# A hybrid S5 / GLA / dilated-attention block on one Trainium2 core: three edits to the order of the work around the gate products

## The chip, the cores and the metric

The kernel runs on one core of one Trainium2 chip. The metric is the device time of one execution in microseconds (us). The core's engines are named as the profile names them: PE is TensorE (matmuls), DVE is VectorE, ACT is ScalarE, POOL is GpSimd and SP is SyncE, which here only starts DMAs. Each engine works through its own list of instructions in order and waits, where it must, for semaphores of the others.

## What is computed

The reference is one transformer block in float32, 1024 tokens of width 1024. The first half of it is what matters here; it mixes three branches:

```python
(u_s5, q_gla, k_gla, v_gla, lr_gla, r_gla, q_att, k_att, v_att, gate_logits) = split(rms_norm(x) @ w_in)
y_a = s5_branch(u_s5, ...)          # state space: per group of 16 channels, 64 complex states, scan over 1024 tokens
y_b = gla_branch(q_gla, ...)        # gated linear attention, 4 heads, chunks of 64
y_c = dilated_branch(q_att, ...)    # windowed attention with dilation 1, 4, 16
gates = sigmoid(gate_logits)        # 1024 x 3 x 1024
merged = sum(gates * einsum('bsnc,ncd->bsnd', stack([y_a, y_b, y_c]), w_branch))
x = x + merged @ w_out
```

Then come cross-attention to 256 memory rows and a squared-ReLU MLP of width 4096, which the change touches only through the stream of weights.

## The kernel before

**Products in split float32.** Large products are made of pairs: each operand is split into a first part (`whi`, `A_hi`), which is the value rounded to the matmul's reduced float32 type, and a second part (`wlo`, `A_lo`), which is what is left. `gemm` (L455) issues three matmuls for each slice of 128 of the contraction: hi x hi, hi x lo, lo x hi. In the profile these are the `m<-A_hi,whi`, `m<-A_lo,whi` and `m<-A_hi,wlo` rows of L151.

**The stream of weights** (`Stream`, L259). `load` (L283) starts on SP's queue the DMA of half a block of weights into one of three buffers `raw`. `begin` queues a block's four quarters. Each call of `tick` (L315) converts one quarter: ACT writes the first part `whi` (L140, scaled by a gain `gk`, or a plain copy at L146), and DVE then writes the second part `wlo` (L137, or L121), which reads what ACT has just written. After every second quarter, `tick` calls `load` for the buffer that came free. `next` finishes whatever quarters of a block are left and begins the following block.

**The clock of the program.** While a large product is issued, `spend` (L440) adds up the matmuls' nominal time. At every 1.28 us of it, one step is taken of each of the side jobs in `sides`, at a rate that each job has; at every second step `ws.tick()` is called. So side jobs are Python generators whose `yield` statements decide how many PE matmuls stand between two of their pieces. Six large matmuls of 512 columns (two slices of the contraction) fill one such step.

**The side jobs in this part of the program.** While the gate products (`gate_evac`, L1230, whose results go to `GT_d` through SP, L1234) run on PE:

- `gla` (from L1031) runs first. It works on pairs of chunks; a table of offsets (`GLA_LV`, `GLA_OUT`) says at which step each piece is issued. `level` makes, for seven levels, an exponential `E`, products `Kt` and `Qt` on DVE and POOL, and PE multiplies `Qt` by `Kt`. `outp` (L1143) makes the result of one chunk: `oc` scales it on DVE, `od` multiplies it by the gate `rg` on POOL, `oe` transposes it on PE, and `of` (L1183) splits it in two parts `e` and stores both to `YB_d` in memory, with DMAs issued by POOL (L1190). The last step of one pair of chunks and the first of the next overlap.
- `p2` waits for `gla` to end and runs `s5b` (L909). It loads `Ug`, the regrouped input, with eight DMAs on SP (L920), and tables (`GTr`, `GTi`, `ctab`, `stab`, `CLr`, `CLi`, `Tz`) with DMAs on POOL (L923). Then come four rounds `qd`. A round multiplies `Ug` by `GTr` and `GTi` on PE (S5's first products), rotates and scans the result on DVE (`Vr`, `Vi`, then `Xr`, `Xi`), waits two steps, and makes the output products: in two halves `q`, each of four `k`, three matmuls with `Tz`, `CLr` and `CLi`, with one `yield` between `k == 1` and `k == 2`. ACT applies the gelu (`Yg`), PE transposes, and ACT and DVE split the result into `GH`.

After the last gate block the program calls `sides.finish(sd_p2)`, which issues all that is left of `s5b` with nothing between, and then starts the next large product, which reads `GH`.

Of the kernel before, what the change touches and what calls it, by code (L numbers as in the profile page):

```python
# [12 lines left out]
ALU = mybir.AluOpType  # L13
# [4 lines left out]
P = 128  # L18
# [67 lines left out]
def body(tc, I, out):  # L86
# [55 lines left out]
    def f(ap):  # L142
        return ap.bitcast(F32)

    def split(hi, lo, src):
        S.copy(hi, src)  # L146
        sub(lo, src, f(hi))
# [114 lines left out]
    class Stream:  # L262
# [3 lines left out]

        def __init__(self):
            self.i = 0
            self.n_load = 0
            self.raw = []  # L270
            self.hl = {}
            self.todo = []

            self.sums, self.n_hi, self.n_lo, self.done, self.started = {}, 0, 0, 0, False
            self.queue7, self.sum_queue, self.parts, self.pair = [], [], {}, None
            self.rows, self.left, self.held, self.n_sum = {}, {}, [], 0
            for x in range(3):
                if x == 2:
                    p0_x(1, SP)
                self.load()  # L280
            self.begin(0)
# [16 lines left out]
        def begin(self, i):  # L298
# [13 lines left out]
            for q in range(4):  # L312
                self.todo.append((hi[:, q * n // 4:(q + 1) * n // 4], lo[:, q * n // 4:(q + 1) * n // 4], q, n // 4, gains[i], k // 4))

        def tick(self):  # L315
            if self.todo:
                hi, lo, q, n, g, nk = self.todo.pop(0)
                raw = self.raw[0][:, q % 2 * n:q % 2 * n + n]
                if g is None:
                    split(hi, lo, raw)  # L320
                else:
                    for k in range(nk):
                        c = slice(k * n // nk, (k + 1) * n // nk)
                        gk = gv[:, g, nk * q + k:nk * q + k + 1]
                        act(hi[:, c], raw[:, c], AF.Copy, scale=gk)
                        stt(lo[:, c], raw[:, c], gk, f(hi[:, c]), ALU.mult, ALU.subtract)
                if q % 2:
                    self.raw.pop(0)
                    self.load()
                return  # L330
            if self.n_lo < len(self.queue7):
                self.tick7()
            elif self.queue7 and self.done >= self.n_lo - 4 and self.i < len(blocks) and not isinstance(gains[self.i], tuple) and self.i not in self.hl:
                self.begin(self.i)
# [574 lines left out]
    def s5b(p, GH):  # L909
# [14 lines left out]
        load(0, ("Ug", "GTr", "GTi", "ctab", "stab"))  # L924
        yield
        load(0, ("CLr", "CLi", "Tz"))
        for _ in range(2):
            yield
        for qd in range(4):
            cur = got[qd]  # L930
            j0 = 4 * qd
            Ug = cur["Ug"]

            SS = []
            load(qd + 1, ("Ug",))
            for l in ("GTr", "GTi"):
                o = qtile([P, 4, P])
                for j in range(4):
                    for x in range(2):
                        mm(o[x * 64:(x + 1) * 64, j, :], cur[l][:, j, x * 64:(x + 1) * 64], Ug[:, 2 * j + x, :])  # L940
                SS.append(o)
                yield
            Sr, Si = SS
            ctab, stab = (cur[n].rearrange("p (a b) -> p a b", a=4) for n in ("ctab", "stab"))
            c1, s1 = ctab[:, :, 1:], stab[:, :, 1:]
            Vr, Vi = T(p, [P, 4, NCH], "Vr"), T(p, [P, 4, NCH], "Vi")
            va, vb = T(ev, [P, 4, NCH], "e1", bufs=2), T(ev, [P, 4, NCH], "e2", bufs=2)
            mul(Vr, Sr, c1)
            mul(vb, Sr, s1)
            mul(va, Si, s1)  # L950
            yield
            add(Vr, Vr, va, eng=G)
            mul(Vi, Si, c1)
            sub(Vi, Vi, vb)
            yield
            load(qd + 1, ("GTr", "GTi"))
            for v in (Vr, Vi):
                for j in range(4):
                    V.tensor_tensor_scan(out=v[:, j, :], data0=rho[:, j0 + j:j0 + j + 1].to_broadcast([P, NCH]),
                                         data1=v[:, j, :], initial=0.0, op0=ALU.mult, op1=ALU.add)  # L960
                yield
            load(qd + 1, ("ctab", "stab"))
            Xr, Xi = T(p, [P, 4, NCH], "Xr"), T(p, [P, 4, NCH], "Xi")
            m = NCH - 1
            c_, s_ = ctab[:, :, 1:NCH], stab[:, :, 1:NCH]
            G.memset(Xr[:, :, 0], 0.0)
            G.memset(Xi[:, :, 0], 0.0)
            mul(va[:, :, :m], Vi[:, :, :m], s_, eng=G)
            mul(vb[:, :, :m], Vi[:, :, :m], c_, eng=G)
            mul(Xr[:, :, 1:], Vr[:, :, :m], c_)  # L970
            mul(Xi[:, :, 1:], Vr[:, :, :m], s_)
            yield
            sub(Xr[:, :, 1:], Xr[:, :, 1:], va[:, :, :m])
            yield
            add(Xi[:, :, 1:], Xi[:, :, 1:], vb[:, :, :m])
            for _ in range(2):
                yield
            Yg = T(p, [P, L5, 8, 16], "Yg")
            CL = [cur[n].rearrange("p (a b) -> p a b", a=4) for n in ("CLr", "CLi")]
            for q in range(2):  # L980
                ps = qtile([P, 4, P])
                o = slice(q * 64, q * 64 + 64)
                for k in range(4):
                    mm(ps[:, k, :], Ug[:, 2 * k + q, :], cur["Tz"][:, 2 * k + q, :], stop=False)
                    mm(ps[:, k, :], Xr[o, k, :], CL[0][o, k, 16:144], start=False, stop=False)
                    mm(ps[:, k, :], Xi[o, k, :], CL[1][o, k, 16:144], start=False)
                    if k == 1:
                        yield
                act(Yg[:, :, q::2, :], ps.rearrange("p k (t c) -> p t k c", t=L5), AF.Gelu_apprx_tanh)
                yield  # L990
            gh = [x[:, qd, :] for x in GH]
            load(qd + 1, ("CLr", "CLi", "Tz"))
            for q in range(2):
                ps = qtile([P, 4, P])
                for k in range(4):
                    tr(ps[:, k, :], Yg[:, 4 * q + k].rearrange("p g c -> p (g c)"))
                hi, lo = (g_.rearrange("p (c t) -> p t c", t=L5)[:, 4 * q:4 * q + 4, :] for g_ in gh)
                split(hi, lo, ps)
                yield
# [46 lines left out]
    def gla(p, B, GQ, GK, GV):  # L1046
# [5 lines left out]
        def tpair(tp, base):  # L1052
# [89 lines left out]
            def outp(t, o0):  # L1142
# [42 lines left out]
                def of():  # L1185
                    hi = T(ev, [P, 4, P], "e1", F32R, bufs=2)
                    lo = T(ev, [P, 4, P], "e2", F32R, bufs=2)
                    split(hi, lo, r["pt"])
                    for x, y in enumerate((hi, lo)):
                        G.dma_start(YB_d[x][:, :, tg * P:(tg + 1) * P], y)  # L1190
                for i, fn in enumerate((oa, ob, oc, od, oe, of)):
                    at(o0 + GLA_OUT[i], fn)
            o0 = GLA_L0 + GLA_SP * 6 + GLA_LV[3] + 1
# [1150 lines left out]
```

## Time and profile before

| | |
|---|---|
| runs shown | 2351.93, 2352.48, 2360.95 us; median 2352.48 us |
| the profiled execution, its own time | 2361.8 us |
| its span, first to last instruction | 2360.0 us |
| PE busy | 2272.0 us, 96% of the span |
| DVE, ACT, POOL busy | 1397.6, 811.0, 635.3 us |
| mean granted clock of PE | 0.976 of full speed |

How to read it: a share of busy time is a mean over stages with different limits. Idle time of PE is what can be gained without removing matmuls, and so is time in which PE is busy at less than its full clock: `PEclk` is the clock granted to TensorE, 1.00 for 2.4 GHz and 0.50 for 1.2 GHz, and a value between them is a mean over a stretch that has both. In a row of the timeline, the brackets hold the idle time of the engine just before the instruction and what ended it.

### The profile page before, as it was taken

The page shows a single profiled execution, that of the slowest core. Times are in us where ns is not written, and L with a number is a line of the kernel's source. Part 1 is how long each engine was busy: PE and PEld are TensorE (multiplying, and loading weights), DVE is VectorE, ACT ScalarE, POOL GpSimd, SP SyncE. Part 2 cuts the span into 40 slices and gives each one's busy share as a digit, 9 for nine tenths or more (in the row PEclk, how much of TensorE's full clock was granted, in tenths as well). Part 3 has the DMA queues.
Part 4 walks back from the last instruction along what each step waited for, and adds up shares of the span by engine and source line. Part 5 has one row for each costly group of instructions (what it writes and reads, how often), then busy time and mean ns, then how long its engine had stood idle before and what let it go on. Part 6 is the DMA issues. An engine that isn't in the chain of part 4 may idle for free.

```text
span 2360.0 us, 31525 instructions
## 1 busy us (share of the span) xinstructions
PE 2272.0 (96%) x11680; PEld 1909.1 (81%) x11680; DVE 1397.6 (59%) x2514; ACT 811.0 (34%) x1777; POOL 635.3 (27%) x589
## 2 busy tenths in 40 slices
PE   9999899999999999999998999999899999999998
PEld 8778777777889888978886889899688888678787
DVE  7886986354542334353347555384577777786674
ACT  5325222112323333323223344263333334343324
POOL 3221444121210000010003320022556563454513
PEclk9999999798999999999999999999899999999999
DMA  5343235441651111141146324101044445354331
GB/s 178 108 147 90 56 88 126 136 122 68 229 157 41 40 45 44 48 90 39 38 115 217 134 66 140 45 10 45 18 147 152 149 153 167 124 177 141 106 103 72
DMA packets 201849, 246.37 MB, mean 104 GB/s; under 512 B 15424, under 2 KB 143072, under 8 KB 201696
## 3 DMA queue, kind: packets, MB, share of 16 engines
q1 hardware_dynamic: 187472, 221.35, 30.2%
q0 software_dynamic: 12640, 18.23, 2.9%
q10 hardware_dynamic: 1584, 4.78, 0.6%
q8 instruction: 92, 1.51, 0.3%
q14 instruction: 61, 0.50, 0.1%
HBM read 179.92 MB, written 64.39 MB: 104 GB/s over the span
## 4 chain that ended last, share of the span: by engine, by line
PE 73%; DVE 14%; DMA 4%; ACT 3%; issue 3%; POOL 2%; SPq 0%; DVEq 0%; ACTq 0%; POOLq 0%
PE m L151 50%; PE q L151 21%; PE q L184 2%; DVE wlo L137 2%; DVE Qt L121 1%; DVE e L121 1%; DMA fm<-ACT_d 1%; DMA wb<-W_d 1%; DVE A_lo L121 1%; POOL b L121 1%; DVE wlo L121 1%; DVE ST L1132 1%; DVE e L137 1%; DVE Kt L121 1%; ACT whi L140 1%
## 5 line engine op out<-in xcount | busy, mean ns | idle before, releaser
L151 PE MATMUL m<-A_hi,whi 128*128 128x512 f32 x1680 | 686.5, 409 | 7.7 <-DVE e L121 7.7
L151 PE MATMUL m<-A_lo,whi 128*128 128x512 f32 x1680 | 665.0, 396 | 7.4 <-POOL A_lo L121 5.2
L151 PE MATMUL m<-A_hi,wlo 128*128 128x512 f32 x1680 | 664.1, 395 | 0.0
L151 PEld LDWEIGHTS m<-A_hi,whi 128*128 128x128 f32 x1680 | 321.4, 191 | 75.4 <-DVE e L121 8.5
L151 PEld LDWEIGHTS m<-A_lo,whi 128*128 128x128 f32 x1680 | 321.8, 192 | 70.5 <-POOL A_lo L121 6.8
L151 PEld LDWEIGHTS m<-A_hi,wlo 128*128 128x128 f32 x1680 | 320.9, 191 | 69.8
L151 PE MATMUL q<-b,whi 128*128 128x512 f32 (+1 forms) x768 | 238.1, 389 | 10.4 <-ACT b L1918 4.1
L137 DVE SCALAR_TENSOR_TENSOR wlo<-raw,gv,whi 128x256 fp32r<-128x256 f32 (+1 forms) x400 | 194.5, 535 | 71.0 <-ACT whi L140 70.6
L140 ACT ACTIVATE whi<-raw,gv 128x256 fp32r<-128x256 f32 (+1 forms) x400 | 174.7, 501 | 174.0 <-PE m L151 141.4
L151 PEld LDWEIGHTS q<-b,whi 128*128 128x128 f32 x768 | 144.3, 191 | 47.3 <-POOL b L121 7.4
L121 DVE TENSOR_TENSOR wlo<-raw,whi 128x512 fp32r<-128x512 f32 x160 | 151.4, 953 | 40.0 <-ACT whi L146 29.7
L121 DVE TENSOR_TENSOR e<-m,RSB 128x512 f32<-128x512 f32 x64 | 50.2, 785 | 166.6 <-PE m L151 160.9
L151 PE MATMUL q<-b,wlo 128*128 128x512 f32 (+1 forms) x384 | 147.5, 384 | 0.0
L121 DVE TENSOR_TENSOR X<-X,q 128x512 f32<-128x512 f32 (+1 forms) x119 | 75.3, 648 | 76.3 <-PE q L151 64.8
L1415 POOL DMA_DIRECT2D ST_d<-s x6 | 3.1, 514 | 400.0 <-ACT s L1414 400.0
L121 POOL TENSOR_TENSOR RSB<-RSB,e 128x512 f32<-128x512 f32 (+1 forms) x53 | 54.6, 1030 | 204.6 <-ACT e L140 204.2
L140 ACT ACTIVATE e<-e 128x512 f32<-128x512 f32 x94 | 59.4, 633 | 137.2 <-DVE e L137 59.3
L151 PE MATMUL m<-whi,A_hi 128*128 128x256 f32 (+1 forms) x328 | 94.1, 287 | 0.0
L151 PE MATMUL m<-whi,A_lo 128*128 128x256 f32 (+1 forms) x328 | 92.9, 283 | 0.0
L151 PE MATMUL m<-wlo,A_hi 128*128 128x256 f32 (+1 forms) x328 | 92.8, 283 | 0.0
L140 ACT ACTIVATE pr<-nl,st 128x128 f32<-128x128 f32 (+1 forms) x96 | 43.3, 451 | 129.8 <-DVE st L1375 129.6
L151 PE MATMUL q<-A_lo,whi 128*128 128x512 f32 (+1 forms) x224 | 84.1, 376 | 3.9 <-POOL A_lo L121 2.6
(397 smaller groups left out, 4242.4 us busy)
## 6 DMA issues: line engine op xcount, KB each, us to landing
raw<-in_w_in_dram SPq DMA_DIRECT2D x48, 512.0 KB
fm<-ACT_d SPq DMA_DIRECT2D x68, 256.0 KB
raw<-in_w_up_dram SPq DMA_DIRECT2D x32, 512.0 KB
raw<-in_w_down_dram SPq DMA_DIRECT2D x32, 512.0 KB
GT_d<-e SPq DMA_DIRECT2D x48, 256.0 KB
raw<-in_w_in_dram SPq DMA_DIRECT2D x48, 256.0 KB
ACT_d<-e SPq DMA_DIRECT2D x48, 256.0 KB
ACT_d<-fm SPq DMA_DIRECT2D x36, 256.0 KB
```

Of the source, the lines that this page charges most:

```text
L121: return eng.tensor_tensor(out=o, in0=a, in1=b, op=op)
L137: return V.scalar_tensor_tensor(out=o, in0=a, scalar=s, in1=b, op0=op0, op1=op1)
L140: return S.activation(o, a, f, **kw)
L151: PE.matmul(o, l, r, start=start, stop=stop, skip_group_check=on_top)
L184: PE.transpose(o, a, ident[:n, :n])
L1132: V.copy_predicated(s["ST"].rearrange("p h (b x n) -> p h b x n", x=2, n=Hh)[:, :, :, 1, :], lmask[:, li * 64:(li + 1) * 64].rearrange("p ...
L1415: G.dma_start(ST_d[ip][g], s2)
```

## The change

Three edits, all in the order in which the same work is issued; no instruction of arithmetic is added or removed.

1. `s5b`: five steps in place of two between the loads and S5's first products; four steps in place of two between the scans and the output products; no step inside a half of the output products.
2. `of`: the two stores to `YB_d` are issued by SP in place of POOL, with both sides seen as plain float32.
3. `Stream.tick`: the second part of a quarter, and the `load` that follows a half block, are put into a list `behind` and issued after the first part of the next quarter. After the last quarter of a block, and in the first blocks (`self.i < 3`), the list is emptied at once.

```diff
         def tick(self):
+
             if self.todo:
+                late, self.behind = self.behind, []
                 hi, lo, q, n, g, nk = self.todo.pop(0)
                 raw = self.raw[0][:, q % 2 * n:q % 2 * n + n]
                 if g is None:
-                    split(hi, lo, raw)
+                    S.copy(hi, raw)
+                    self.behind.append(lambda: sub(lo, raw, f(hi)))
                 else:
                     for k in range(nk):
...
                         act(hi[:, c], raw[:, c], AF.Copy, scale=gk)
-                        stt(lo[:, c], raw[:, c], gk, f(hi[:, c]), ALU.mult, ALU.subtract)
+                        self.behind.append(lambda c=c, gk=gk: stt(lo[:, c], raw[:, c], gk, f(hi[:, c]), ALU.mult, ALU.subtract))
+                        if self.i < 3:
+                            self.flush()
                 if q % 2:
                     self.raw.pop(0)
-                    self.load()
+                    self.behind.append(self.load)
+                for fn in late:
+                    fn()
+                if self.i < 3 or not self.todo:
+                    self.flush()
                 return
...
         load(0, ("CLr", "CLi", "Tz"))
-        for _ in range(2):
+        for _ in range(5):
             yield
...
             add(Xi[:, :, 1:], Xi[:, :, 1:], vb[:, :, :m])
-            for _ in range(2):
+            for _ in range(4):
                 yield
...
                     mm(ps[:, k, :], Xi[o, k, :], CL[1][o, k, 16:144], start=False)
-                    if k == 1:
-                        yield
                 act(Yg[:, :, q::2, :], ps.rearrange("p k (t c) -> p t k c", t=L5), AF.Gelu_apprx_tanh)
...
                     for x, y in enumerate((hi, lo)):
-                        G.dma_start(YB_d[x][:, :, tg * P:(tg + 1) * P], y)
+                        SP.dma_start(f(YB_d[x][:, :, tg * P:(tg + 1) * P]), f(y))
```

How this moves instructions shows on three engines. First DVE's list in the first round of `s5b`, from the rotation to the first correction of `Xr`. Before:

```order
L121 TENSOR_TENSOR e_590_4138<-q_4092,stab_4047 128x512
L121 TENSOR_TENSOR e_589_4137<-q_4113,stab_4047 128x512
L137 SCALAR_TENSOR_TENSOR wlo_4059<-raw_3858,gv_82,whi_4058 128x256 x2
L121 TENSOR_TENSOR Vi_4136<-q_4113,ctab_4045 128x512
L121 TENSOR_TENSOR Vi_4136<-Vi_4136,e_590_4138 128x512
L959 SCALAR_TENSOR_TENSOR Vr_4135<-rho_155,Vr_4135 128x128 x4
L137 SCALAR_TENSOR_TENSOR wlo_4059<-raw_3858,gv_82,whi_4058 128x256 x2
L959 SCALAR_TENSOR_TENSOR Vi_4136<-rho_155,Vi_4136 128x128 x4
L121 TENSOR_TENSOR e_594_4188<-m_4131,RSB_91 128x512
L121 TENSOR_TENSOR Xr_4199<-Vr_4135,ctab_4045 128x4x127
L121 TENSOR_TENSOR Xi_4200<-Vr_4135,stab_4047 128x4x127
L121 TENSOR_TENSOR Xr_4199<-Xr_4199,e_589_4137 128x4x127
```

After the change, from the start of the rotation:

```order
L121 TENSOR_TENSOR Vr_4160<-q_4122,ctab_4045 128x512
L121 TENSOR_TENSOR e_591_4163<-q_4122,stab_4047 128x512
L121 TENSOR_TENSOR e_590_4162<-q_4137,stab_4047 128x512
L121 TENSOR_TENSOR e_592_4173<-m_4100,RSB_91 128x512
L121 TENSOR_TENSOR Vi_4161<-q_4137,ctab_4045 128x512
L121 TENSOR_TENSOR Vi_4161<-Vi_4161,e_591_4163 128x512
L973 SCALAR_TENSOR_TENSOR Vr_4160<-rho_155,Vr_4160 128x128 x4
L973 SCALAR_TENSOR_TENSOR Vi_4161<-rho_155,Vi_4161 128x128 x4
L121 TENSOR_TENSOR Xr_4214<-Vr_4160,ctab_4045 128x4x127
L121 TENSOR_TENSOR Xi_4215<-Vr_4160,stab_4047 128x4x127
L121 TENSOR_TENSOR e_600_4228<-m_4176,RSB_91 128x512
L121 TENSOR_TENSOR Xr_4214<-Xr_4214,e_590_4162 128x4x127
```

The two pairs of `wlo` have left the stretch between rotation and `Xr`; six of them now stand ahead of it, and the `e<-m` rows (gate results taken out of PSUM) fall at other places.

Next PE's list at the end of `s5b`, from the last output product of the fourth round to the first product that reads `GH`. Before:

```order
L151 MATMUL q_4974<-CLi_4790,Xi_4913 128x128
L151 MATMUL m_4946<-A_hi_101,whi_4536 128x512
L151 MATMUL m_4946<-A_lo_102,whi_4536 128x512
L151 MATMUL m_4946<-A_hi_101,wlo_4537 128x512
L151 MATMUL m_4946<-A_hi_101,whi_4536 128x512
L151 MATMUL m_4946<-A_lo_102,whi_4536 128x512
L151 MATMUL m_4946<-A_hi_101,wlo_4537 128x512
L184 MATMUL q_5003<-ident_84,Yg_4950 128x128 x4
L184 MATMUL q_5010<-ident_84,Yg_4950 128x128 x4
L151 MATMUL m_5026<-GH_567_4027,whi_4782 128x512
```

After the change:

```order
L151 MATMUL q_4989<-CLr_4806,Xr_4927 128x128
L151 MATMUL q_4989<-CLi_4808,Xi_4928 128x128
L184 MATMUL q_5003<-ident_84,Yg_4974 128x128 x4
L184 MATMUL q_5010<-ident_84,Yg_4974 128x128 x4
L151 MATMUL m_5026<-GH_567_4027,whi_4753 128x512
```

The six gate matmuls between the last output product and the transposes (`q<-ident,Yg`) are gone from there, and all 24 output products of that round stand in one run. In the first three rounds the list now has 66 gate matmuls in place of 57 between S5's first products and the output products (60 in the fourth), two runs of 12 output products with 6 gate matmuls between them in place of four runs of 6 with 3, 6 and 6 between, and 18 gate matmuls more ahead of the very first product of `s5b`.

Last SP's list where `gla` ends and `s5b` begins. Before:

```order
L1234 DMA GT_d_122<-e_553_3933 128x512
L1161 DMA rg_3940<-RG_d_120 128x512
L1234 DMA GT_d_122<-e_562_3989 128x512
L920 DMA Ug_4032<-U_d_121 16x8x128 x8
L1234 DMA GT_d_122<-e_574_4055 128x512
L920 DMA Ug_4083<-U_d_121 16x8x128 x8
```

After the change:

```order
L1246 DMA GT_d_122<-e_562_3989 128x512
L1202 DMA YB_d_28_123<-e_565_4016 512x1x128
L1202 DMA YB_d_29_124<-e_566_4017 512x1x128
L934 DMA Ug_4032<-U_d_121 16x8x128 x8
L1246 DMA GT_d_122<-e_574_4055 128x512
```

The stores of the last chunk now stand directly ahead of the first loads of `Ug`, and the second set of `Ug` loads has moved further back. POOL's list loses these stores and goes from the multiplication by `rg` straight to the loads of the tables.

## Rows read from the trace of the kernel before

**Rows 1.** Windows by stretch: length, busy us of each engine (count), PEclk, DMA share, GB/s.
```profile
228.00:244.00 16.00, 12.96 (x106) 12.38 (x106) 13.54 (x27) 5.39 (x11) 4.70 (x6) 1.00 0.23 65
280.00:300.00 20.00, 15.15 (x73) 12.25 (x72) 19.05 (x27) 4.37 (x15) 11.73 (x15) 0.91 0.42 97
325.00:345.00 20.00, 15.79 (x72) 12.83 (x71) 17.73 (x24) 4.79 (x9) 11.64 (x15) 0.83 0.35 71
370.00:380.00 10.00, 7.31 (x38) 5.75 (x37) 9.26 (x14) 1.94 (x4) 5.53 (x7) 1.00 0.45 95
410.00:425.00 15.00, 11.21 (x60) 8.51 (x60) 2.70 (x6) 3.31 (x8) 2.40 (x5) 0.77 1.01 263
435.00:465.00 30.00, 28.57 (x93) 21.99 (x93) 5.57 (x7) 4.73 (x7) 3.10 (x4) 0.60 0.24 79
480.00:500.00 20.00, 18.56 (x96) 14.64 (x95) 5.95 (x8) 2.59 (x5) 4.35 (x5) 1.00 0.30 90
515.00:545.00 30.00, 28.57 (x91) 22.01 (x91) 6.31 (x9) 1.72 (x3) 4.41 (x5) 0.60 0.24 80
560.00:580.00 20.00, 19.60 (x101) 15.56 (x100) 6.63 (x10) 2.53 (x4) 3.31 (x3) 1.00 0.16 58
```

**Rows 2.** Timeline of PE ahead of S5's first product: start us, us, instruction.
```profile
412.32 0.39 PE L151 MATMUL m<-A_lo,whi 128*128 128x512 f32 x1
412.55 0.39 PE L151 MATMUL m<-A_hi,wlo 128*128 128x512 f32 x1
416.72 0.69 PE L151 MATMUL q<-Ug,GTr 128*64 128x128 f32 x4 [3.79 <-DMA Ug<-U_d]
```

**Rows 3.** Waits of PE, 400 to 560 us: total us, times, longest.
```profile
PE q L151 <- DVE Xr L121: 4.0, 3, 1.3
```

**Rows 4.** Timeline of PE at the first output products of S5's first round.
```profile
435.95 0.38 PE L151 MATMUL q<-Tz,Ug 128*128 128x128 f32 x2
437.65 0.49 PE L151 MATMUL q<-CLr,Xr 64*128 64x128 f32 x2 [1.32 <-DVE Xr L121]
```

**Rows 5.** Timeline of DVE between rotation and Xr in that round.
```profile
426.97 1.91 DVE L137 SCALAR_TENSOR_TENSOR wlo<-raw,gv,whi 128x256 fp32r<-128x256 f32 x2
...
431.41 0.86 DVE L137 SCALAR_TENSOR_TENSOR wlo<-raw,gv,whi 128x256 fp32r<-128x256 f32 x2
```

**Rows 6.** Waits of DVE, 200 to 395 us.
```profile
DVE wlo L137 <- ACT whi L140: 11.9, 16, 1.2
```

**Rows 7.** Timeline of all engines where two pairs of GLA's chunks meet.
```profile
284.24 0.68 DVE L121 TENSOR_TENSOR e<-q,gst 128x512 f32<-128x512 f32 x1
...
285.85 1.55 POOL L1190 DMA_DIRECT2D YB_d<-e  x2 [1.82 <-ACT e L146]
...
286.78 4.66 DVE L121 TENSOR_TENSOR Kt<-E,GK 128x256 f32<-128x256 f32 x1
...
287.27 1.42 POOL L121 TENSOR_TENSOR e<-e,rg 128x512 f32<-128x512 f32 x1
...
288.74 0.66 PE L184 MATMUL q<-ident,e 128*128 128x128 f32 x4 [1.20 <-POOL e L121]
...
289.74 1.40 POOL L121 TENSOR_TENSOR e<-GQ,GK 128x512 f32<-128x512 f32 x1
...
292.35 0.98 PE L151 MATMUL q<-Qt,Kt 128*128 128x128 f32 x4 [2.95 <-DVE Qt L121]
```

**Rows 8.** Timeline of SP's queue: the first loads of Ug.
```profile
405.53 4.67 SPq L920 DMA_DIRECT2D Ug<-U_d  x8
```

**Rows 9.** Timeline of DVE: the second part of GLA's last result.
```profile
406.79 0.69 DVE L121 TENSOR_TENSOR e<-q,e 128x512 fp32r<-128x512 f32 x1 [1.78 <-ACT e L146]
```

**Rows 10.** Timeline of POOL: last multiplication by rg.
```profile
402.85 1.37 POOL L121 TENSOR_TENSOR e<-e,rg 128x512 f32<-128x512 f32 x1
```

**Rows 11.** Timeline of ACT: the last gelu of S5.
```profile
576.65 0.60 ACT L140 ACTIVATE Yg<-q 128x512 f32<-128x512 f32 x1 [6.34 <-PE q L151]
```

**Rows 12.** The page's fifth part, conversion of weights on ACT: idle before, releasers.
```profile
L140 ACT ACTIVATE whi<-raw,gv 128x256 fp32r<-128x256 f32 (+1 forms) x400 | 174.7, 501 | 174.0 <-PE m L151 141.4
```

More of the change, by code (lines that the diff above doesn't have):

```diff
@@ L268, in __init__ @@
             self.i = 0
+            self.behind = []
             self.n_load = 0
@@ L313, in begin, with flush @@
                 self.todo.append((hi[:, q * n // 4:(q + 1) * n // 4], lo[:, q * n // 4:(q + 1) * n // 4], q, n // 4, gains[i], k // 4))
+        def flush(self):
+            while self.behind:
+                self.behind.pop(0)()
         def tick(self):
             if self.todo:
+                late, self.behind = self.behind, []
                 hi, lo, q, n, g, nk = self.todo.pop(0)
```

## The prediction

> **What bounds the kernel now.** PE is busy for 96% of the span, so I looked first for the stretches in which it is not, or in which its clock is below 2.4 GHz, and then for what ended its waits there. Windows of 5 us over the whole trace led to the stretches in [rows 1]. In each I take as lost the length less busy time times mean clock; that is rough where idle time and a low clock fall together. The gate stage has two parts. While GLA's side job runs, 228 to 244 loses 3.0 us, 280 to 300 loses 20 - 15.15 x 0.91 = 6.2, 325 to 345 loses 6.9, and 370 to 380 loses 2.7. While S5's side job runs, 410 to 425 loses 6.4, 435 to 465 loses 30 - 28.57 x 0.60 = 12.9, 480 to 500 loses 1.4, 515 to 545 loses 12.9 and 560 to 580 loses 0.4. That is 18.8 us and 34.0 us; the change works on just these.
>
> In S5 the causes are short waits. PE stands 3.79 us for `Ug` [rows 2], and in rounds one to three 4.0 us in all for `Xr` [rows 3], 1.32 of it in the first round [rows 4]. The larger part is the clock that follows. In the first and third rounds it fell to 1.2 GHz a few us after the wait and stayed there while output products ran; after the same loss of 1.4 us in the second round, and with 0.4 us in the fourth, it stayed at 2.4 GHz [rows 1].
>
> **S5's first products.** They move back by 18 gate matmuls. One gate matmul follows the other after 0.23 us [rows 2], so PE arrives 4.1 us later, against a wait of 3.79. But the load moves too. Its eight DMAs started at 405.53 [rows 8]; now two stores stand ahead of them, and the second of these needs DVE's result of 406.79 + 0.69 = 407.48 [rows 9]. With about 0.58 us for one DMA's issue (4.67 / 8), `Ug` would start some 3.1 us later, and at worst 3.79 + 3.1 - 4.1 = 2.8 us of wait stay. In favour: POOL no longer waits for the same result between its multiplication, which ends at 404.22 [rows 10], and its seven table loads. Those transfers filled the DMA engines in 410 to 425 (share 1.01 [rows 1]), which is why `Ug` came late. They now leave earlier, and the second set of `Ug` leaves later. I take the wait as gone, and the lost clock of the stretch with it: 6.4 us; the other end is 1.0.
>
> **The output products.** Rounds one to three get nine more gate matmuls ahead of them, 2.1 us, against waits of 1.3 us. DVE's way to `Xr` also loses two pairs of `wlo`, 1.91 + 0.86 = 2.8 us [rows 5], whose place ahead of the rotation is one where DVE waits for PE anyway. So the waits should be gone with 3 us to spare: 4.0 and the fourth round's 0.4, with the bounds 4.4 and 3. Losing the step inside a half costs no arithmetic, but the output products now stand in runs of 12. Whether the clock then holds is the largest open term: 12.9 - 1.4 = 11.5 us for each of two rounds, 23.0 in all. Its ends are 23.0 saved, and 23.0 lost if the second and fourth rounds fall too. I take 23.0 saved, because the nearest row is 480 to 500: four runs of six, a loss of 1.4 us ahead, and clock 1.00 throughout.
>
> **The end of S5.** The fourth round now finishes with nothing between its pieces. The six gate matmuls that stood over the last gelu are used up earlier, so PE waits for that gelu: 0.60 us [rows 11] and the hand-over, which I put at 0.3 from what stands between such rows; 0.9 lost, between 0.6 and 2. Splitting `GH` was exposed before and stays so.
>
> S5 together: 6.4 + 12.9 + 12.9 + 1.4 + 0.4 - 0.9 = 33.1 us.
>
> **Second parts behind the next first part.** Between 200 and 395 us DVE stood 11.9 us, 16 times, for the first part that ACT was still writing [rows 6]. That is about 0.75 each, four times in 228 to 244, where DVE is the engine that PE waits for: 3.0 lost by PE there, four times 0.75 removed. With a quarter's second part behind the next quarter's first, ACT is done when DVE comes to it. I take all of 3.0; the ends are 1 and 3.0. Elsewhere I cost the edit at nothing. A second part is late by one tick, two steps, and conversion runs ahead: ACT's longest waits are for PE to release the buffer of the block before (141.4 of 174.0 us [rows 12]). If that cover were gone, a `raw` buffer could come late, at 1 to 3 us in a place where blocks are short.
>
> **Stores on SP.** Sixteen issues leave POOL. The price of one is seen where two pairs of chunks meet [rows 7]. DVE's result for POOL is ready at 284.24 + 0.68 = 284.92, but POOL waits for ACT's and DVE's parts, issues the two stores, and multiplies only from 287.27. From there it runs four instructions without a gap until 291.14. DVE's `Kt`, begun at 286.78, takes 4.66 us in all that time and ends 0.30 us behind POOL's run, and PE waits 1.20 and then 2.95 us. Without the stores the run begins 2.35 us earlier and so does all that follows: PE's 4.15 become 1.8. The two other meetings look the same, so 7.0 us. Their clock, 1.3 + 2.7 = 4.0, should then hold, as it did in 370 to 380 with 2.7 us idle. Together 11.0. The lower end is nothing, if the run of POOL only meets other work of DVE; the upper is all of the three windows, 15.8.
>
> As the Trainium skill has it (SBUF — State Buffer, section "SBUF: two separate sides"), VectorE with two inputs in SBUF and GpSimd exclude each other for a whole instruction, whichever starts first. If VectorE came in after the one instruction, it would have been out for no more than 1.42 us here, and only the waits of 1.20 would be saved: 3.6 in place of 7.0, and 2318. The row of 4.66 us says that the whole run of four holds it out.
>
> SP's own time costs nothing as long as it idles; what stands behind the stores there is weighed below.
>
> **Sum.** 33.1 + 3.0 + 11.0 = 47.1 us. Against the profiled execution's own 2361.8 that is 2314.7, so **2315**. That execution is 9.3 us above the median of the runs shown and near the highest of them (2360.95); against the median the forecast is a gain of 37 us.
>
> **Rivals.**
> - *The clock still falls in some rounds.* For it: `CLr` and `CLi` use half of the rows (64*128 [rows 4]), only 6 gate matmuls stand between the runs in place of 15 in a round, and in 435 to 465 the clock didn't come back until these products ended. Against it: no wait precedes them. 11.5 us a round: 2326 for one, 2338 for two. Chance 0.18.
> - *It falls in all four rounds, and the kernel is slower.* The same place and price, now caused by the runs of 12 alone: 2315 + 46 = 2361, above the median of before; with `Ug` late and the lower end of the stores it passes 2364. It decides from the fourth round on (three give 2349). Chance 0.05.
> - *DVE is held out as long as before.* POOL's run starts earlier, but only the 1.20 waits go: 11.0 becomes about 3.6, so 2322; with nothing gained, 2326. Chance 0.12.
> - *SP holds `Ug` back.* The stores wait on SP, and all loads behind them too: 2.8 us of wait and 2.6 of clock stay, 2320. Chance 0.04. The Trainium skill (DMA: Bandwidth & Descriptors, section "Anatomy of one DMA — SWDGE (gpsimd) path") says that a DMA's wait for a semaphore happens on the issuing sequencer before dispatch. By that rule this rival is certain to delay the start of `Ug`; the two times of [rows 8, 9] show the order, and not the outcome.
> - *Nothing moves the end*, because what PE saves it waits for at the next block of weights: 2352. Chance 0.03.
>
> **How the numbers follow.** The forecast has 0.58, from 2309 (all 52.8 us of the windows) to 2322. The range reaches from 2305, 4 us lower for what the third edit may save outside the windows, to 2338, two rounds at the low clock. Half a percent, about 12 us, is what a measurement of this kernel can tell from no change. Faster by more than that is below 2340.7: the forecast, most of the first rival, the third and fourth, 0.88 after taking off a little for prices that I may have wrong together. Within it 0.09, slower 0.03.
>
> **What would show it.** Right: no PE wait for `Xr`, and at most 1 us for `Ug`; clock 1.00 through S5's four rounds; DVE's waits for `whi` in the GLA part down from 11.9 to under 4 us; DVE's longest `Kt` or `Qt` under 3 us; a new PE wait of about 1 us ahead of S5's last transposes. Wrong: a clock of 0.5 inside the runs of 12 without a wait ahead; `Kt` still at 4.6 us; PE waiting for `raw` or `wlo`.

## The result, and the profile after

The changed kernel takes **2321.67 us** (median of four executions, 2317.44 to 2324.36) against 2353.8 us before (four, 2351.93 to 2360.95): ratio 0.9848, 95% interval 0.9826 to 0.987. That is faster by 1.5%, inside the forecast's range and 6.7 us above its 2315. The executions that left the two profiles took 2361.8 and 2317.4 us: 44.4 us apart, where the sum had said 47.1.

The windows that answer to [rows 1] lie up to 40 us earlier now (columns as there):

```profile
228.00:244.00 16.00, 15.20 (x130) 15.02 (x129) 15.82 (x33) 4.13 (x8) 6.82 (x9) 1.00 0.23 67
274.00:294.00 20.00, 17.39 (x102) 14.48 (x101) 19.10 (x33) 6.34 (x18) 10.55 (x13) 1.00 0.40 127
313.00:333.00 20.00, 17.34 (x100) 14.44 (x99) 19.14 (x32) 6.34 (x18) 10.61 (x13) 1.00 0.41 127
353.00:365.00 12.00, 10.73 (x57) 8.66 (x57) 11.13 (x22) 3.19 (x12) 6.22 (x8) 1.00 0.45 132
398.00:413.00 15.00, 12.54 (x78) 9.79 (x77) 6.51 (x13) 0.63 (x2) 3.54 (x7) 1.00 0.92 250
420.00:440.00 20.00, 20.00 (x115) 15.79 (x114) 4.71 (x7) 7.42 (x12) 1.65 (x3) 1.00 0.24 82
455.00:475.00 20.00, 20.00 (x115) 15.52 (x115) 5.39 (x9) 6.68 (x12) 1.64 (x3) 1.00 0.25 83
488.00:508.00 20.00, 20.00 (x115) 15.78 (x114) 4.50 (x7) 5.57 (x8) 1.65 (x3) 1.00 0.25 83
520.00:540.00 20.00, 19.31 (x94) 15.53 (x93) 5.86 (x7) 6.16 (x8) 1.19 (x2) 0.91 0.07 26
```

S5's first three rounds lose nothing: PE is busy for the whole window at clock 1.00, where two rounds before lost 12.9 us each. The meetings of GLA's chunks lose 2.6, 2.7 and 1.3 us in place of 6.2, 6.9 and 2.7. What is left in S5 is 2.46 us ahead of its first products and 20 - 19.31 x 0.91 = 2.4 us at its end.

The waits of PE, 400 to 560 us (against [rows 3]), and DVE's wait for the first part, 200 to 395 us (against [rows 6]):

```profile
PE q L151 <- DMA GT_d<-e: 2.5, 1, 2.5
PE q L184 <- ACT Yg L140: 0.7, 1, 0.7
...
DVE wlo L137 <- ACT whi L140: 0.8, 1, 0.8
```

No wait for `Xr` is left, and DVE's 11.9 us for `whi` are 0.8. The first row names a store, but the waiting matmul reads `Ug` and `GTr`, and `GTr` and `GTi` had landed by 396.3; so it waits for `Ug`. SP's queue (columns: start, us) and SP's own waits, 388 to 412 us, tell why:

```profile
392.07 1.24 SPq L1202 DMA_DIRECT2D YB_d<-e  x2
393.49 8.97 SPq L934 DMA_DIRECT2D Ug<-U_d  x8
402.57 0.84 SPq L1246 DMA_DIRECT2D GT_d<-e  x2
...
404.77 1.09 PE L151 MATMUL q<-Ug,GTr 128*64 128x128 f32 x16 [2.46 <-DMA GT_d<-e]
```

```profile
SPq L934 <- DMA YB_d<-e: 2.6, 2, 2.2
```

The two stores are issued, then the eight loads of `Ug`, which need 8.97 us to issue where they needed 4.67 [rows 8]. Of these, 2.6 us are waits of SP: by this row the seventh and the eighth load stand until the two stores ahead of them are done. PE arrives at 404.77 - 2.46 = 402.31 and waits. But from the first load's issue to the first product it is 11.28 us here, and it was 416.72 - 405.53 = 11.19 before [rows 2, 8]: `Ug` needs no longer than it did. What moved is the time that PE leaves it: PE now arrives 8.82 us after the first issue, and 7.40 before.

Where the first two pairs of chunks meet, DVE and POOL (against [rows 7]):

```profile
279.36 0.68 DVE L121 TENSOR_TENSOR e<-q,gst 128x512 f32<-128x512 f32 x1
280.12 1.29 POOL L121 TENSOR_TENSOR e<-e,rg 128x512 f32<-128x512 f32 x1 [0.96 <-DVE e L121]
...
281.37 0.74 POOL L121 TENSOR_TENSOR Kt<-E,GK 128x256 f32<-128x256 f32 x1
281.91 0.49 DVE L121 TENSOR_TENSOR Kt<-E,GK 128x256 f32<-128x256 f32 x1
282.07 0.80 POOL L121 TENSOR_TENSOR E<-B 128x256 f32<-128x256 f32 x1
282.32 2.26 DVE L121 TENSOR_TENSOR Qt<-E,GQ 64x256 f32<-64x256 f32 x2
282.83 1.46 POOL L121 TENSOR_TENSOR e<-GQ,GK 128x512 f32<-128x512 f32 x1
```

POOL multiplies 0.08 us after DVE's result is ready (279.36 + 0.68), where it took 2.35 us before. `Kt` takes 0.49 us in place of 4.66.

### The profile page after: what moved, and what is told of

The parts are those of the page before. It is cut to its first block, busy times and chain, and to the rows that moved or that the text cites. A ratio compares the mean times of both kernels' runs of the same rounds, so it can differ in the third digit from the quotient of the medians.

```text
span 2315.7 us, 31549 instructions
## 1 busy us (share of the span) xinstructions
PE 2241.2 (97%) x11680; PEld 1888.9 (82%) x11680; DVE 1383.6 (60%) x2514; ACT 811.0 (35%) x1777; POOL 627.8 (27%) x573
## 5 line engine op out<-in xcount | busy, mean ns | idle before, releaser
L151 PE MATMUL m<-A_hi,whi 128*128 128x512 f32 x1680 | 678.3, 404 | 9.3 <-DVE e L121 9.3
L151 PE MATMUL m<-A_lo,whi 128*128 128x512 f32 x1680 | 658.1, 392 | 6.8 <-POOL A_lo L121 3.5
L151 PEld LDWEIGHTS m<-A_hi,whi 128*128 128x128 f32 x1680 | 317.7, 189 | 74.6 <-DVE e L121 10.2
L137 DVE SCALAR_TENSOR_TENSOR wlo<-raw,gv,whi 128x256 fp32r<-128x256 f32 (+1 forms) x400 | 188.7, 525 | 14.2 <-ACT whi L140 14.1
```

The lines of the kernel that those rows point to most:

```text
L137: return V.scalar_tensor_tensor(out=o, in0=a, scalar=s, in1=b, op0=op0, op1=op1)
L151: PE.matmul(o, l, r, start=start, stop=stop, skip_group_check=on_top)
```

## The experiments

Ratios are to the kernel before, run beside each group (medians 2358.25, 2361.68 and 2358.51 us of 17, 7 and 9 executions), with 95% intervals. The four kernels with ratios to 2361.68 ran on another chip, and the changed kernel was not among them: they compare with it through the ratios (0.9848 and 0.9842 for the changed kernel). "Lost" is length less busy time times clock, as in the prediction.

### The parts alone

S5's steps alone (the first edit):

```diff
-        for _ in range(2):
+        for _ in range(5):
...
-            for _ in range(2):
+            for _ in range(4):
...
-                    if k == 1:
-                        yield
```

> The kernel before with the steps of S5 alone (five steps, four steps, none inside a half); stores on POOL and second parts as before. Theory: the three edits work on separate stretches and their gains add. Between 400 and 585 us the kernel before lost 34.8 us to waits and low clock, the changed one 4.7, so this kernel gains 28 to 32 us against the profiled execution of before: ratio 0.986 to 0.989. The wait for Ug is gone or under 1 us, because POOL's stores, not SP's, stand ahead of the tables; no wait for Xr in rounds one to three; clock 1.00 there. The three meetings of GLA's chunks stay as before (18.8 us lost from 228 to 380). Rival: the second parts of weights, still between rotation and Xr on DVE, keep PE waiting for Xr for 0.5 us or more a round, and the dense runs of output products behind that wait lose the clock in one round or more: gain 7 to 20 us, ratio 0.991 to 0.997.

Measured 2329.97 us, ratio 0.9885 (0.9868 to 0.9901), as the theory had it: no wait for `Xr`, clock 1.00 in the rounds, 0.5 us for `Ug`, the meetings as before.

The stores alone (the second edit):

```diff
-                        G.dma_start(YB_d[x][:, :, tg * P:(tg + 1) * P], y)
+                        SP.dma_start(f(YB_d[x][:, :, tg * P:(tg + 1) * P]), f(y))
```

> The kernel before with the sixteen stores of GLA's result on SP alone. Theory: the meetings of two pairs of chunks lose 6.5 us in place of 15.8, no product Kt or Qt on DVE is over 2.5 us, and their clock stays at 1.00; but SP's loads of Ug now wait behind two stores and PE comes to S5's first products 4.1 us earlier than in the changed kernel, so its wait for Ug grows from 3.8 to 6 or 7 us. Net gain 5 to 9 us, ratio 0.996 to 0.998. Rival: the products on DVE became short because second parts of weights left its list there, not because of the stores; then the longest Kt stays at 4.6 us, the meetings lose 13 us or more, and with the longer wait for Ug the kernel is equal or slower, ratio 1.000 to 1.002.

Measured 2352.46 us, ratio 0.9977 (0.9963 to 0.9991). The three meetings of chunks (windows):

```profile
280.00:295.00 15.00, 12.36 (x67) 9.87 (x66) 14.21 (x24) 3.34 (x7) 8.58 (x10) 1.00 0.35 103
320.00:335.00 15.00, 12.36 (x69) 10.16 (x68) 13.82 (x21) 4.16 (x8) 7.96 (x10) 1.00 0.30 91
355.00:365.00 10.00, 8.68 (x50) 6.96 (x48) 9.15 (x19) 2.77 (x11) 5.47 (x7) 1.00 0.52 155
```

The waits of PE, 200 to 600 us:

```profile
PE q L151 <- DMA Ug<-U_d: 6.8, 1, 6.8
```

The theory held. The meetings lose 2.6, 2.6 and 1.3 us, as in the whole change: the stores, not the second parts, cause that gain. The wait for `Ug` grows from 3.8 to 6.8 us, the other side of the same edit.

The second parts alone (the third edit; the core of its diff stands ahead of the prediction):

```diff
-                        stt(lo[:, c], raw[:, c], gk, f(hi[:, c]), ALU.mult, ALU.subtract)
+                        self.behind.append(lambda c=c, gk=gk: stt(lo[:, c], raw[:, c], gk, f(hi[:, c]), ALU.mult, ALU.subtract))
```

> The kernel before with the second parts (and loads) of a quarter behind the next quarter's first part, alone. Theory: DVE's wait for the first part falls from 11.9 us to under 2 us between 200 and 395 us, 228 to 244 loses 0.8 in place of 3.0 us, and the meetings of chunks lose about as much as before (15 to 16 us); S5's waits for Xr shrink by what the second parts took from DVE's way (2.8 us), so they vanish, and the clock of one or two of S5's rounds may hold without the other edit: gain 2 to 3 us, or 13 to 26 us if one or both rounds are kept. Rival: S5's waits stay, because DVE waits for other things ahead of Xr; then the gain is 2 to 3 us, ratio 0.999, and the waits for Xr are 1.0 us or more each.

**A miss.** Measured 2367.16 us, ratio 1.0049 (1.0032 to 1.0066): slower. DVE's row between the two scans of the first round (timeline), and PE's waits for `Xr` in the four rounds (waits, 400 to 600 us):

```profile
427.89 1.65 DVE L137 SCALAR_TENSOR_TENSOR wlo<-raw,gv,whi 128x256 fp32r<-128x256 f32 x4
```

```profile
PE q L151 <- DVE Xr L121: 7.2, 4, 2.1
```

Four `wlo` now stand there, where there were two (0.86 us, [rows 5]). The late list adds to DVE's way to `Xr`, and each of the first three waits grows from 1.32 to 2.1 us; the clock fell in the second, third and fourth round, and held in the first. In the whole change the `wlo` left that place because S5's added steps moved it; with S5's steps alone none stands there either.

The whole change without its third edit:

```diff
-                        self.behind.append(lambda c=c, gk=gk: stt(lo[:, c], raw[:, c], gk, f(hi[:, c]), ALU.mult, ALU.subtract))
+                        stt(lo[:, c], raw[:, c], gk, f(hi[:, c]), ALU.mult, ALU.subtract)
```

> The changed kernel without its third edit: S5's steps and stores on SP, second parts right behind their first parts as before. Alone the third edit made the kernel slower by 0.5%, through longer waits for Xr; with S5's steps there are none. Theory: in the whole change it is worth the 2.2 us that 228 to 244 lost more before (3.0 against 0.8): this kernel takes 2 to 4 us more than the changed one, with no wait for Xr, clock 1.00 in S5's rounds, and meetings of chunks that lose 6.5 us. Rival: the third edit costs time elsewhere (later loads of weights), and this kernel is 2 to 8 us faster than the changed one.

Measured 2322.36 us beside 2322.19 for the changed kernel on the same chip. The stretch 228 to 244 lost 3.0 us in place of 0.8, as said, but the time does not show it; whether the third edit is worth 2 us in the whole is not settled. With S5's steps in place no harm of it can be measured either.

So the gains of the three edits do not add, against the first of these theories: alone they bring 28.3, 5.8 and -8.9 us, together 25.2, and the whole change 32 to 36.

### What differs from one execution to the next

The kernel before, once more:

> The kernel before once more, for a second profile. Its runs lie between 2351.9 and 2361.0 us and the profiled one was near the top. Theory: the spread comes from TensorE's clock in a few stretches, S5's rounds among them: an execution near 2352 us has one round of S5 (11.5 us) or about as much elsewhere at the high clock, while the waits of PE are the same within 1 us in total. Rival: the spread comes from waits for memory late in the program (merge, attention, MLP), and both S5 rounds and GLA's meetings lose the same as in the first profile, within 1 us.

Its execution took 2355.6 us. The waits for `Xr` were the same (1.32, 1.31, 1.31 and 0.28 us). Windows around the four rounds' output products:

```profile
430.00:450.00 20.00, 18.57 (x70) 14.44 (x69) 6.64 (x11) 1.88 (x2) 2.77 (x2) 0.74 0.23 73
470.00:495.00 25.00, 23.57 (x88) 18.18 (x87) 6.79 (x11) 1.20 (x2) 3.99 (x5) 0.73 0.18 59
515.00:535.00 20.00, 18.57 (x72) 14.22 (x71) 3.43 (x5) 1.20 (x2) 2.17 (x3) 0.74 0.09 33
555.00:575.00 20.00, 18.89 (x96) 14.60 (x96) 6.60 (x9) 5.48 (x7) 0.74 (x2) 1.00 0.08 27
```

The first three rounds fell here, and each for a shorter time: they lose 6.3, 7.8 and 6.3 us, against 12.9, 1.4 and 12.9. From 410 to 585 us this execution lost 28.5 us by windows of 5 us, the first 35.7; their times differ by 6.2. So the same waits bring different losses from one execution to the next, as the theory had it, though no round of the first three kept its clock here. In the runs the time goes with the mean clock: nine further executions of before lie between 2353.7 us at 0.980 and 2369.0 us at 0.972.

### The wait or the density

The step inside a half put back, three steps ahead (runs of six, no wait in rounds one to three):

```diff
-            for _ in range(4):
+            for _ in range(3):
...
+                    if k == 1:
+                        yield
```

> The changed kernel with the step inside a half of the output products put back (runs of six) and three steps in place of four ahead of them. Question: does the clock hold in S5 because no wait stands ahead of the output products, or because they stand in denser runs? Theory (the wait decides): rounds one to three show no wait for Xr over 0.3 us and clock 1.00 as in the changed kernel. The four steps more than in the changed kernel use up gate products, so the fourth round has 42 in place of 60 ahead of its output products and waits 3 to 5 us for Xr there: 2325 to 2332 us. Rival (density decides): the clock falls in one or more of rounds one to three though nothing waits: 6 to 13 us more for each, 2335 us or over.

Measured 2332.54 us, ratio 0.9872 (0.985 to 0.9894), a hair above the theory's span. Rounds one to three (the first shown; the others read alike) and four:

```profile
420.00:440.00 20.00, 20.00 (x103) 15.99 (x102) 4.46 (x7) 4.48 (x8) 3.28 (x5) 1.00 0.15 54
...
522.00:545.00 23.00, 20.05 (x75) 15.76 (x74) 5.78 (x11) 2.15 (x4) 3.75 (x3) 0.67 0.07 24
```

Without a wait the spread-out runs keep the clock. The fourth round, ahead of which 42 gate products stand in place of 60, waits 2.3 us and falls.

Two steps in place of four (runs of twelve, waits back):

```diff
-            for _ in range(4):
+            for _ in range(2):
```

> The changed kernel with two steps in place of four ahead of the output products: the wait for Xr comes back, the runs of twelve stay, and 36 gate products more cover the end of S5. Theory (the wait decides, as in the kernel before, where waits of 1.3 us went ahead of every fall): PE waits 0.5 to 1.3 us for Xr in rounds one to four, and the clock falls in one to four of them; 6 to 13 us for each, so 2330 to 2365 us. Rival (dense runs keep the clock): waits of the same size, clock 1.00 in all four rounds; only the waits are lost and the end is gained, 2321 to 2326 us.

Measured 2330.28 us, ratio 0.9866 (0.9845 to 0.9888). Rounds one, two and three:

```profile
420.00:435.00 15.00, 15.00 (x83) 11.82 (x82) 2.35 (x4) 4.40 (x6) 1.74 (x4) 1.00 0.18 53
450.00:475.00 25.00, 24.66 (x90) 19.12 (x89) 5.00 (x6) 2.29 (x3) 4.13 (x5) 0.66 0.21 71
488.00:510.00 22.00, 20.36 (x98) 15.88 (x96) 8.12 (x11) 3.35 (x4) 4.24 (x5) 0.92 0.28 94
```

The first has no wait and holds; the second waits 0.23 us and falls; the third waits 1.52 and falls for a shorter time; the fourth waits 0.78 and holds. So dense runs do fall. The first and the third have the same list on PE, 54 gate products ahead of the two runs and 9 between them: what tells them apart is the wait.

Three steps, with the first `CLr`, `CLi`, `Tz` later in the program:

```diff
-        load(0, ("Ug", "GTr", "GTi", "ctab", "stab"))
-        yield
-        load(0, ("CLr", "CLi", "Tz"))
-        for _ in range(5):
+        load(0, ("Ug", "GTr", "GTi", "ctab", "stab"))
+        for _ in range(6):
             yield
+        load(0, ("CLr", "CLi", "Tz"))
...
-            for _ in range(4):
+            for _ in range(3):
```

> As the kernel with the tables later, and with three steps in place of four ahead of the output products, so that gate products stand over the end of the fourth round again (six between its output halves and its transposes). Theory: the wait for Ug goes (2.5 us); the end loses 0.8 us in place of 2.3; the Xr waits stay away, because the second parts of weights have left the way to Xr (slack about 3 us, a step is 1.4): 2317 to 2319 us against the changed kernel's 2321.7. Rival: the wait for Xr comes back with 0.3 us or more, and the clock falls in a round: 2325 to 2335 us.

Measured 2326.48 us, ratio 0.9842 (0.9817 to 0.9867), the ratio of the changed kernel in place of a gain: the rival came in the fourth round, with less wait than it named. Its first product after the wait (timeline of PE), and the window around them:

```profile
520.01 0.49 PE L151 MATMUL q<-CLr,Xr 64*128 64x128 f32 x2 [0.20 <-DVE Xr L121]
```

```profile
515.00:540.00 25.00, 24.69 (x89) 19.18 (x88) 6.43 (x10) 2.30 (x3) 3.31 (x3) 0.67 0.13 43
```

0.20 us of wait, and 25 - 24.69 x 0.67 = 8.5 us lost. All rounds of all 14 profiles of this study together, by the wait for `Xr` or `Xi` that stands ahead of or in the output products:

| wait | rounds | clock fell during the output products |
|---|---|---|
| none | 35 | 0 |
| 0.20 to 0.29 us | 5 | 2 |
| 0.78 to 2.3 us | 16 | 13 |

A wait ahead makes the fall likely and does not decide it: 6 of the 21 rounds with a wait kept the clock, one of them behind 2.11 us. What decides among these is open.

### The wait for `Ug` that is left

The changed kernel once more, as the measure for what follows:

> The changed kernel once more, on the same chip as the next three, as their measure. Theory (the spread is TensorE's clock in stretches where PE waits): S5's first three rounds have clock 1.00 and no wait again; the median lies between 2318 and 2325 us. Rival: one round of S5 loses its clock in some executions, 6 to 12 us: a median above 2327 or single runs above 2332.

Measured 2322.19 us (2319.99 to 2323.11), S5's output products at 1.00 in all rounds; the wait for `Ug` 2.61 us. The theory held.

The later place of the three tables by itself, with four steps ahead of the output products:

```diff
-        yield
-        load(0, ("CLr", "CLi", "Tz"))
-        for _ in range(5):
+        for _ in range(6):
             yield
+        load(0, ("CLr", "CLi", "Tz"))
```

> The changed kernel with the first loads of CLr, CLi and Tz (1.1 MB) issued after the six steps ahead of S5's first products in place of after the first step. Question: is the wait of 2.46 us for Ug that is left in the changed kernel due to the two stores ahead of it on SP, or to the tables that fill the DMA engines at the same time? Theory (the tables): SP's eight loads of Ug, 8.97 us from first to last issue in the changed kernel, take under 6 us, and the wait falls under 0.5 us: 2 to 2.5 us gained, 2319 us, and no new wait for Tz or CLr, which are needed 20 us later. Rival (the stores on SP): Ug's issues begin at the same place and the wait stays over 1.5 us; time unchanged.

Measured 2324.9 us, ratio 0.9837 (0.9814 to 0.9859), wait 2.4 us. It tells the two theories apart in nothing, for the loads did not move. The last of them on POOL, in the changed kernel and in this one:

```profile
393.00 0.53 POOL L937 DMA_DIRECT2D Tz<-Tz_d  x1
```

```profile
393.49 0.53 POOL L937 DMA_DIRECT2D Tz<-Tz_d  x1
```

POOL has nothing to wait for between these loads, and goes through the list at once; a later place in the program is not a later time.

The three tables on SP, behind the loads of `Ug`, where SP's own issues hold them back:

```diff
-                G.dma_start(t, s5_d[n][qd])
+                (SP if qd == 0 and n in ("CLr", "CLi", "Tz") else G).dma_start(t, s5_d[n][qd])
```

> The changed kernel with the first loads of CLr, CLi and Tz (1.1 MB) on SP, behind the eight loads of Ug and one store of a gate result, in place of POOL, where the kernel with the tables later in the program started them at the same time as the changed kernel. Theory A (the tables fill the DMA engines): Ug is there 2 us or more earlier after its first issue than the 11.3 us of the changed kernel, PE's wait of 2.46 falls under 0.5. Theory B (what counts is that SP starts Ug 2.7 us later against PE than before, behind the two stores): 11.3 us from first issue to first product stay, within 1 us, and so does the wait. The time moves by 2.5 us at most, under what a run can tell; a load of weights that now stands behind the tables on SP could cost 1 to 3 us.

**2317.77 us** (2314.14 to 2319.14), ratio 0.9822 (0.9799 to 0.9845); each of its four executions is below each of the changed kernel's four beside it. It beats the kernel before and, in this group, the changed kernel.

```profile
392.83 5.27 SPq L934 DMA_DIRECT2D Ug<-U_d  x8
...
401.58 1.09 PE L151 MATMUL q<-Ug,GTr 128*64 128x128 f32 x16
```

```profile
SPq L934 <- DMA YB_d<-e: 0.9, 2, 0.6
```

SP issues the loads in 5.27 us, and the product starts 8.75 us after the first of them without a wait. So the tables did hold `Ug` up: theory A. The two stores still stand ahead on SP, but the last two loads now wait 0.9 us for them in place of 2.6 (waits of SP, 388 to 412 us); a part of what the tables cost came through these stores. Some 2.6 us of the 4.4 gained are that wait; the rest is spread over the program and was not followed.

The last chunk's two stores back on POOL:

```diff
+                        if tg == 7:
+                            G.dma_start(YB_d[x][:, :, tg * P:(tg + 1) * P], y)
+                        else:
-                        SP.dma_start(f(YB_d[x][:, :, tg * P:(tg + 1) * P]), f(y))
+                            SP.dma_start(f(YB_d[x][:, :, tg * P:(tg + 1) * P]), f(y))
```

> The changed kernel with the two stores of the last chunk alone back on POOL; the other fourteen stay on SP. Theory B: SP starts Ug 2 to 3 us earlier against PE's arrival, and the wait of 2.46 us falls to 0 to 0.7 us (0.5 in the kernel with S5's steps alone, where all stores are on POOL); the meetings of chunks keep their 6.5 us of loss, for none of them has these two stores. 2319 to 2320 us. Theory A (tables against Ug): POOL's tables start later too, behind DVE's result, so the wait shrinks as well, but then the time from first issue to first product falls under 10 us; with B it stays near 11. If the wait doesn't shrink both are wrong.

Measured 2319.67 us (2316.06 to 2320.54), ratio 0.9829 (0.9806 to 0.9853). SP starts `Ug` earlier, POOL the tables later:

```profile
389.70 4.46 SPq L934 DMA_DIRECT2D Ug<-U_d  x8
...
392.69 0.72 POOL L937 DMA_DIRECT2D GTr<-GTr_d  x1
...
401.18 1.09 PE L151 MATMUL q<-Ug,GTr 128*64 128x128 f32 x16
```

PE doesn't wait, so 11.48 us from first issue to product is only an upper bound. The packets in the traces say more (512 bytes each, on SP's queue): the last one of these eight loads ends 9.7 us after the first issue here, 10.2 in the changed kernel and 7.0 with the three tables behind `Ug`. So with tables and stores on POOL, 3 us behind, the loads take nearly as long as in the changed kernel; most of what removed the wait here is that SP starts `Ug` 2.7 us earlier against PE's arrival, as theory B had it. Both causes count: with less traffic beside the loads the wait goes, and with an earlier start it goes too.

## Why the prediction was right, and where its terms were off

| term | put at | measured |
|---|---|---|
| first products | 6.4 | 6.4 - 2.46 = 3.9 |
| output products, four rounds | 27.6 | 27.6 |
| the end of S5 | -0.9 | 0.8 - 2.4 = -1.6 |
| second parts | 3.0 | 3.0 - 0.8 = 2.2 |
| stores | 11.0 | 15.8 - 6.5 = 9.3 |
| sum | 47.1 | 41.4 |

The two profiled executions differ by 44.4; the other 3 us lie outside these stretches, in no term of the sum, and bring the total nearer to the forecast than its terms are.

- **Output products**: right, and by the mechanism that was named. The short waits for `Xr` went, and with them the fall of the clock. My doubt, that runs of twelve alone would bring it down, was answered by 32 rounds of dense runs without a wait that all held. But the rival of a falling clock was closer than its 0.18 says: of the five rounds with 0.20 to 0.29 us of wait, two fell.
- **First products**: the step that failed is "I take the wait as gone". The rows had given 2.8 us, and 2.46 stayed. What I set against them (the tables leave POOL earlier, so the DMA engines are free) brought nothing. Before, the tables started 3 us after `Ug`; now the first of them starts at 389.71, nearly 4 us ahead of it, and from first issue to product it is 11.28 us in place of 11.19. PE came 4.1 us later, but `Ug` started 2.7 us later in the same list, and of the 3.79 us only 1.3 went. In its wait the rival *SP holds `Ug` back* came true, with a chance of 0.04 beside it; the clock did not fall there. That was luck: in three of the other kernels, with 2.3 to 2.6 us of the same wait, it fell for a few us (0.91 over 400 to 420 us, 1.00 here).
- **The end of S5**: the wait for the gelu was 0.69 us, near the 0.6 from the row; but the transposes, too, have no cover now, and the clock came down to 0.80 and 0.86 in the two pieces of 5 us there. Of that clock nothing was in the term. The 0.8 us is a wait for `GH` just behind S5, in 580 to 585 us before, which is gone in this execution. In four of the later kernels with the same end the clock held, and a wait of 0.7 us for `GH` stayed.
- **Second parts**: right in size for DVE's waits (11.9 to 0.8 us) and nearly so for PE; what was not seen is that the edit alone lengthens DVE's way to `Xr`. The 2.8 us of `wlo` that the prediction took off that way belong to the first edit.
- **Stores**: right to 2 us, and their gain is shown by the second edit alone. The step behind it, that POOL's whole run holds DVE out, is not general. After the change the same four POOL instructions run from 280.12 to 284.29 without a gap, yet DVE's `Kt` gets in with 0.49 us, and only the pair of `Qt` is long (2.26 us, where the shortest such pairs take 0.84). The Trainium skill (SBUF — State Buffer, section "SBUF: two separate sides") has the two engines exclude each other for one instruction. With that the row after the change agrees, for `Kt` and each of the two `Qt` end 0.28 or 0.29 us behind the end of one POOL instruction, and the 4.66 us over four instructions in [rows 7] does not. By it the prediction would have had 7.6 of the 11 us (3.6 in place of 7.0), and the rival without the clock 3.6; 9.3 came. Why `Kt` stayed out in [rows 7] is open; it began at 286.78, while POOL was still issuing its two stores (285.85 to 287.40), and after the change no store stands there.

Against the median the forecast was a gain of 37 us. The four executions of before that stand beside the result give 32; a later group of nine gives 2358.51 - 2322.19 = 36.3. The profiled execution of after was the lowest of its four, that of before above the highest of its four, which makes their distance larger than that of the medians.

## What to carry over

Price a short wait of PE with the clock that it may bring down: in S5 waits of 1.3 us cost up to 12.9 us with the clock behind them. No round without a wait lost it, and two of five with 0.20 to 0.29 us did, so a wait that is only made short can still cost. When a load moves to another queue or another neighbour in one, add up from the rows when it starts against when it is needed, and believe the sum before a reason that speaks against it. A test of an edit alone says what it does alone: the third edit cost 0.5% by itself, and nothing that could be measured in company.

## What the runs showed that was not expected

- A wait of 0.20 us ahead of S5's output products was followed by a loss of 8.5 us, nearly all of it at the low clock, while waits of 0.78, 1.32 and 2.11 us were each followed once by no fall.
- Moving three loads five steps later in the program changed their start on POOL by 0.49 us, about what that whole stretch was later in that execution (`Ug` by 0.45): an engine with nothing to wait for runs ahead of the program's steps.
- Eight loads of 64 KB issued from SP took 4.46 to 4.79 us where the tables started about 3 us behind them, and 8.4 to 9.0 us where the tables had started nearly 4 us ahead and two stores stood ahead on SP, with 2.3 to 2.7 us of it spent on waits for these stores. Still, wherever PE waited, it was 11.0 to 12.0 us from first issue to product in both cases: the time to issue did not tell when `Ug` was there.
